# Attention of a hybrid transformer layer put in the program's own order, with steps and copies moved between places and engines

## Chip, cores and metric

The kernel runs on one core of a Trainium2 chip. The number that counts is the time of one execution on the device, in microseconds (us). Each kernel is also run once under the hardware profiler; the profile's times are from that one execution. The engines are PE (TensorE, matmuls and transposes), DVE (VectorE), ACT (ScalarE), POOL (GpSimd) and SP, which here only issues DMAs. Each engine takes its own instructions one after the other and waits for others by semaphores.

## The reference

One layer: a modulated RMSNorm, a projection to two groups of heads (attention, and a gated MLP over chunks), an output projection with a gated residual, then a mixture of 16 experts. All is fp32. The part that matters here is the attention over 1024 latent and 256 context tokens, 8 query heads in 2 groups of 4 that share a key and value head of 64 columns:

```python
def block(qb):
    s = jnp.einsum('bqkgd,bskd->bkgqs', qb, k).astype(jnp.float32) * scale
    p = jax.nn.softmax(s, axis=-1).astype(v.dtype)
    return jnp.einsum('bkgqs,bskd->bqkgd', p, v)
...
mix_l = jnp.concatenate([gqa_attend(ql, k_all, v_all),
                         spatial_gating(hl, w_gm, v_gain, w_s, b_s)], axis=-1)
xl_new = xl + gt1 * (mix_l @ w_out)
```

## The kernel before

Products are made from fp32 values split in two parts that PE multiplies apart: a high part (`whi`, `ph`: a rounded copy) and a low part (`wlo`, `pl`: the value less the high part). A split is a copy on ACT or DVE and a subtraction on DVE or POOL.

The queries of all heads are computed first. Then the attention runs over 16 **units** `u`: 8 blocks of 128 queries, 2 groups of 4 heads each. A unit has 10 **steps** `kt`, one for each 128 of the 1280 keys. Step `i = 10 u + kt` of the loop at L827 holds:

- `scores` (L740): two matmuls into the PSUM tile `st` (L745, L746), 128 keys by 512 columns (4 heads of 128 queries), the exponential on ACT into `pf` (L748, four buffers), and the two parts of the probabilities: `ph`, a copy on ACT (L751) or DVE (L753), and `pl`, a subtraction on POOL (L755).
- up to three pieces of `head(u + 1)` (L628), the preparation of the next unit. It is a generator, and each `yield` ends a piece. For the first group of a block it doubles the queries into the tile `qd` (L634; here called QD); four transposes turn them (L640, tile `tp`); ACT copies the result to `QA` (L643, one of the tiles named HL), DVE subtracts to `QB` (L644). Then the maximum of the scores of each query is found: 8 products of 512 keys (L652) and 4 half ones (L659) into the PSUM tile `ap`, which has two buffers, each followed by a maximum on DVE (L654, L662); L665 takes the maximum over all, four transposes (L669) turn it into a row, and ACT copies it (L671) where the second score matmul of the next unit (L746) reads it, so that the maximum is subtracted in the product.
- `values` (L758) of the step five earlier (`LAG`): six matmuls of 256 columns (L768) into the PSUM tile `po`, which also hold the sums of the probabilities. After a unit's last one it is divided: two copies on ACT (L773, L774), a reciprocal (L775) and two products (L777, L778) on DVE.
- `next(side)`: from unit 3 on and every sixth step, a piece of the work for the stages behind: `gates` (L726), and `w_out` (L782), which loads a quarter of the out-projection's weights into `raw`, multiplies 128 rows by the gate (L789 on DVE) and splits them (L147 on ACT, L148 on DVE). The last quarter is multiplied only.

The order of instructions is set in two ways. The stage before the attention and the stages after it stand in a `manual_schedule`: each engine gets its instructions in the order in which the program issues them. The attention doesn't: there a scheduler places the instructions of every engine before the run. The rotation of the last block of queries (L840) is tied behind the first reciprocals by `issue_after`.

Of the kernel before, what the change touches and what calls it, by code (L numbers as in the profile page):

```python
# [47 lines left out]
def layer(ctx: ExitStack, tc: tile.TileContext, a, out, dbg=None):  # L48
# [69 lines left out]
    QD = [kvp.tile([P, NQ, 2, HD], F32, name="qd")]  # L118
# [430 lines left out]
    def q_gain(t):  # L549
        if t < NT - 1:  # L550
            qn = pq_.tile([P, NQ, HD], F32, name="vv", bufs=2)
        else:

            qn = pb_.tile([P, 512], F32, name="pf", bufs=4).rearrange("p (h d) -> p h d", h=NQ)
            qst["tmp"] = None
        qst[t] = qn
        if 3 <= t < NT - 1:
            for h in range(NQ):
                nc.scalar.activation(qn[:, h], ps[2 * NT + t][:, h * HD:(h + 1) * HD], AF.Copy,
                                     scale=qst["ss", t][:, h:h + 1])  # L560
        else:
            nc.vector.tensor_tensor(qn, ps[2 * NT + t].rearrange("p (h d) -> p h d", h=NQ),
                                    qst["ss", t].unsqueeze(2).to_broadcast([P, NQ, HD]), op=OP.mult)

    def q_rotate(t):
        qn = qst[t]
# [5 lines left out]
        ts = qst["tmp"][:, 512:1024] if t < NT - 1 else pb_.tile([P, 512], F32, name="pf", bufs=4)  # L572
        tv = ts.rearrange("p (h s i) -> p h s i", h=NQ, s=2)
        nc.vector.tensor_tensor(dv, xv, cosG[:, t, None].to_broadcast([P, NQ, 2, 32]), op=OP.mult)
        for i in range(2):
            nc.vector.tensor_tensor(tv[:, :, i, :], xv[:, :, 1 - i, :],
                                    sinG[:, t, None, 1 - i].to_broadcast([P, NQ, 32]), op=OP.mult)
        nc.vector.tensor_sub(dv[:, :, 0, :], dv[:, :, 0, :], tv[:, :, 0, :])
        nc.vector.tensor_add(dv[:, :, 1, :], dv[:, :, 1, :], tv[:, :, 1, :])

    for t in range(NT):
        s = 2 * NT + t
        at(s + 1, 0, q_norm, t)
        if t < NT - 1:
            at(s + 1, 4, q_gain, t)
            at(*((s + 1, 7) if t == NT - 2 else (s + 2, 1)), q_rotate, t)
# [41 lines left out]
    def head(u, psum, tags):  # L628
# [3 lines left out]
        if g == 0:  # L632
            qd = QD[0]
            nc.vector.tensor_copy(qd, qall[t].rearrange("p (h d) -> p h d", h=NQ).unsqueeze(2).to_broadcast(  # L634
                [P, NQ, 2, HD]))
            yield
        qd = QD[0]
        pq = ptile(0)
        for s, h in enumerate(HORD):
            nc.tensor.transpose(pq[:, s * P:(s + 1) * P], qd[:, g * QPK + h].rearrange("p a d -> p (a d)"), ident)  # L640
# [74 lines left out]
    psB = pool("psB", 1, space=PSUM)  # L715
    gt1b = pb_.tile([P, D], F32, name="gt1b")
# [23 lines left out]
    def scores(u, kt):  # L740
# [8 lines left out]
        ph = pb_.tile([P, 512], F32R, name="ph", bufs=LAG + 1)  # L749
        if kt in PH_ACT or (u == 0 and kt == 0):  # L750
            nc.scalar.copy(ph, pf)  # L751
        else:
            nc.vector.tensor_copy(ph, pf)  # L753
        pl = pb_.tile([P, 512], F32R, name="pl", bufs=LAG + 1)
        (nc.vector if kt in PL_DVE else nc.gpsimd).tensor_tensor(pl, pf, ph.bitcast(F32), op=OP.subtract)  # L755
        return ph, pl

    def values(u, k, ph, pl):  # L758
# [11 lines left out]
        if k == NK - 1:  # L770
            del U["po", u], U[u]
            rec = pb_.tile([P, 256], F32, name="rec", bufs=1)
            nc.scalar.copy(rec[:HD], po[HD:, 0:256])  # L773
            nc.scalar.copy(rec[HD:], po[:HD, 256:512])  # L774
            U["rec"] = nc.vector.reciprocal(rec, rec)  # L775
            dst = qall[t][:, g * 256:(g + 1) * 256]
            nc.vector.tensor_mul(dst[:HD], po[:HD, 0:256], rec[:HD])  # L777
            nc.vector.tensor_mul(dst[HD:], po[HD:, 256:512], rec[HD:])  # L778
# [3 lines left out]
    def w_out(cb, jh, later=None):  # L782
# [18 lines left out]
    PL_DVE, PH_ACT = (), (0, 2, 4, 5, 6, 8)  # L801
# [24 lines left out]
    C_AT = 12  # L826
    for i in range(NU * NK + LAG):  # L827
        u, kt = divmod(i, NK)
        if i < NU * NK:
            if kt == 0:  # L830
                nxt = head(u + 1, psB, (("tp", 2), ("ap", 2))) if u + 1 < NU else iter(())
            parts[i] = scores(u, kt)
            for _ in range(3 if kt < NK - 1 else 99):
                if next(nxt, 0) == 0:
                    break
        if u >= 3 and i % 6 == 0:
            next(side, None)
        if i == LAG + NK:
            with tc.issue_after(U["rec"].ins):
                q_rotate(NT - 1)  # L840
        if i >= LAG:
            values(*divmod(i - LAG, NK), *parts.pop(i - LAG))
        if i >= NU * NK - C_AT and (i - NU * NK + C_AT) % 2 == 0 and i < NU * NK - C_AT + 8:
            c_load(0, 1 + (i - NU * NK + C_AT) // 2)
    for _ in side:
        pass
    for t in range(NT):
        dump(f"o{t}", qall[t])
    psB.release()
# [755 lines left out]
```

## Time and profile before

| | before |
|---|---|
| time, median of 3 runs | 1797.2 us (1794.7 to 1797.37) |
| the profiled execution | 1797.9 us |
| its span, first to last instruction | 1795.7 us |
| mean granted clock of TensorE | 0.986 |
| PE, DVE, ACT, POOL busy, share of the span | 96%, 89%, 69%, 28% |

A row of a timeline gives start and duration, engine, the line of the kernel, the operation, what it writes and reads, and in brackets the time that its engine stood idle before it and what ended that. "PEld" is the load of a matmul's weights, which runs beside the matmul before it. In groups the number behind the bar is busy time in us and the mean of one in ns, and then the idle time before. Matmuls overlap: the distance of their starts, not their duration, is what one costs PE.

### The profile page before, as it was taken

What the parts mean: (1) busy time and instruction counts of PE and PEld (TensorE: products, weight loads), DVE (VectorE), ACT (ScalarE), POOL (GpSimd) and SP (SyncE); (2) the same over time, 40 slices, a digit from 0 to 9 for tenths busy, and PEclk for the clock granted to TensorE, in tenths of its full rate; (3) what the DMA queues carried; (4) which work ended last, traced back from release to release, by engine and by line L of the source; (5) the groups of instructions that cost most, each with busy time, mean ns of one, the idle gap of its engine ahead of it and who ended that gap; (6) DMA issues with size and microseconds to landing.
All of it is one profiled execution on the core that took longest, in us unless ns stands there. A gap on an engine that the chain in (4) does not pass through costs nothing.

```text
span 1795.7 us, 24620 instructions
## 1 busy us (share of the span) xinstructions
PE 1721.7 (96%) x8636; PEld 1417.9 (79%) x8636; DVE 1591.4 (89%) x2390; ACT 1246.4 (69%) x1675; POOL 507.3 (28%) x349
## 2 busy tenths in 40 slices
PE   7999999889999969999999999999999999999997
PEld 4888878778888858777778888888888888888885
DVE  7778788997758999999999999999999999999987
ACT  6542367657753348777777888887887888878875
POOL 1433468778851112333330110110101101101002
PEclk9999999899999989999999999999999999999999
DMA  9347200100025678999999999999999999999982
GB/s 352 100 154 233 81 1 1 47 1 1 13 95 204 230 270 317 348 365 365 345 371 379 392 382 383 388 380 382 387 385 377 387 385 373 390 383 377 376 303 94
DMA packets 204684, 484.65 MB, mean 270 GB/s; under 512 B 10416, under 2 KB 12816, under 8 KB 204560
## 3 DMA queue, kind: packets, MB, share of 16 engines
q1 hardware_dynamic: 200096, 466.83, 70.2%
q0 software_dynamic: 4464, 16.25, 3.6%
q8 instruction: 67, 1.10, 0.2%
q14 instruction: 57, 0.47, 0.1%
HBM read 462.60 MB, written 20.45 MB: 269 GB/s over the span
## 4 chain that ended last, share of the span: by engine, by line
PE 81%; DVE 12%; issue 2%; ACT 1%; POOL 1%; DMA 1%; POOLq 0%; DVEq 0%; ACTq 0%
PE p L1480 24%; PE p L1483 12%; PE py L1470 6%; PE py L1469 6%; PE py L1471 6%; PE po L768 4%; DVE wlo L148 3%; PE pj L691 2%; PE pj L693 2%; PE pj L692 2%; PE tp L1316 2%; PE ap L652 2%; PE st L746 2%; PE st L745 1%; PE pj L956 1%
## 5 line engine op out<-in xcount | busy, mean ns | idle before, releaser
L148 DVE TENSOR_TENSOR wlo<-raw,whi 128x1024 fp32r<-128x1024 f32 (+1 forms) x561 | 663.2, 1224 | 46.1 <-ACT whi L147 41.9
L147 ACT CAST whi<-raw 128x1024 fp32r<-128x1024 f32 (+1 forms) x595 | 597.4, 1020 | 124.0 <-PE p L1483 67.8
L755 POOL TENSOR_TENSOR pl<-pf,ph 128x512 fp32r<-128x512 f32 x160 | 215.2, 1362 | 59.0 <-DVE ph L753 23.5
L1480 PE MATMUL p<-whi,xb 128*128 128x512 f32 x512 | 204.9, 400 | 0.0
L1480 PE MATMUL p<-whi,xa 128*128 128x512 f32 x512 | 204.7, 400 | 0.0
L1480 PE MATMUL p<-wlo,xa 128*128 128x512 f32 x512 | 199.9, 390 | 0.0
L1480 PE MATMUL p<-wlo,xb 128*128 128x512 f32 x512 | 199.8, 390 | 0.0
L1470 PE MATMUL py<-wlo,thl 128*128 128x512 f32 x504 | 198.3, 394 | 0.0
L1469 PE MATMUL py<-whi,thl 128*128 128x512 f32 x504 | 197.6, 392 | 0.0
L1471 PE MATMUL py<-whi,thl 128*128 128x512 f32 x504 | 196.3, 389 | 0.0
L1483 PE MATMUL p<-whi,xb 128*128 128x512 f32 x512 | 158.1, 390 | 0.4 <-DVE xb L1436 0.4
L1483 PE MATMUL p<-whi,xa 128*128 128x512 f32 x512 | 158.0, 390 | 0.0
L748 ACT ACTIVATE pf<-st 128x512 f32<-128x512 f32 x160 | 95.4, 598 | 73.3 <-PE st L746 58.7
L148 DVE TENSOR_TENSOR wlo<-H,whi 128x1024 fp32r<-128x1024 f32 x104 | 129.1, 1267 | 8.5 <-ACT whi L147 7.5
L148 DVE TENSOR_TENSOR wlo<-gm,whi 128x1024 fp32r<-128x1024 f32 x108 | 130.5, 1229 | 5.7 <-ACT whi L147 5.3
L147 ACT CAST whi<-H 128x1024 fp32r<-128x1024 f32 x108 | 113.8, 1055 | 24.4 <-PE p L1483 18.5
L147 ACT CAST whi<-gm 128x1024 fp32r<-128x1024 f32 x108 | 112.8, 1053 | 16.3 <-PE py L1471 8.4
L1334 POOL DMA_INDIRECT acc<-ye,idx x15 | 38.1, 2539 | 289.8 <-DVE ye L1331 289.8
L1483 PEld LDWEIGHTS p<-whi,xb 128*128 128x128 f32 x512 | 96.0, 188 | 21.6 <-DVE xb L1436 0.8
L1483 PEld LDWEIGHTS p<-whi,xa 128*128 128x128 f32 x512 | 96.1, 188 | 20.9
L1469 PEld LDWEIGHTS py<-whi,thl 128*128 128x128 f32 x504 | 94.6, 188 | 21.5
L1480 PEld LDWEIGHTS p<-wlo,xa 128*128 128x128 f32 x512 | 96.3, 188 | 18.9 <-DVE wlo L148 0.4
(410 smaller groups left out, 3716.0 us busy)
## 6 DMA issues: line engine op xcount, KB each, us to landing
raw<-in_w_dram SPq DMA_DIRECT2D x272, 1024.0 KB, 8.2
H<-in_w_dram SPq DMA_DIRECT2D x54, 1024.0 KB, 7.8
gm<-in_w_dram SPq DMA_DIRECT2D x54, 1024.0 KB, 8.7
raw<-in_w_mod_dram SPq DMA_DIRECT2D x64, 256.0 KB, 3.2
raw<-in_w_mod_dram SPq DMA_DIRECT2D x4, 1024.0 KB, 7.6
raw<-in_w_in_dram SPq DMA_DIRECT2D x16, 256.0 KB, 3.7
raw<-in_w_out_dram SPq DMA_DIRECT2D x4, 1024.0 KB, 5.0
xr<-in_x_dram SPq DMA_DIRECT2D x8, 512.0 KB, 6.0
```

The costliest lines, as they stand in the source:

```text
L147: nc.scalar.copy(hi, src)
L148: (eng or nc.vector).tensor_tensor(lo, src, hi.bitcast(F32), op=OP.subtract)
L652: nc.tensor.matmul(pa_, QA[:, h * P:(h + 1) * P], K1[:, g, pp * 512:(pp + 1) * 512], start=True, stop=True)
L748: nc.scalar.activation(pf, pst, AF.Exp, scale=HD ** -0.5)
L755: (nc.vector if kt in PL_DVE else nc.gpsimd).tensor_tensor(pl, pf, ph.bitcast(F32), op=OP.subtract)
L768: nc.tensor.matmul(po[:, sl], st[:, blk], mv[:, sl], start=(k == 0 and o == 0 and n == 0), stop=(k == NK - 1 and n == 2), skip_group_check ...
L1334: nc.gpsimd.indirect_dma_start(out=acc, out_offset=bass.IndirectOffsetOnAxis(ap=idx[:, e:e + 1], axis=0), in_=G["ye"], in_offset=None, com ...
L1469: nc.tensor.matmul(PY[e][cb], th, hi[:, sl], start=fst, stop=False)
L1470: nc.tensor.matmul(PY[e][cb], th, lo[:, sl], start=False, stop=False)
L1471: nc.tensor.matmul(PY[e][cb], tl, hi[:, sl], start=False, stop=lst)
L1480: nc.tensor.matmul(p, xh[:, j, :], w[:, jj, :], start=(j == 0 and w is pr[0]), stop=False)
L1483: nc.tensor.matmul(p, xl[:, j, :], pr[0][:, jj, :], start=False, stop=(j == DJ - 1))
```

## The change

- The attention gets a `manual_schedule` (mB): on every engine the order is now the program's.
- `halves` is cut off from `scores` and is called one step later. `ph` is copied on ACT in eight steps of ten where it was six, and `ph` and `pl` have five buffers each where they had six.
- `head` copies QD on ACT, and ends a piece behind the copy of QA.
- The division is a generator `divide`, in three pieces: ACT's copies, the reciprocal a step later behind the head's pieces, the two products another step later.
- `side` has the last rotation of queries in front (four pieces), is called every fourth step from unit 1 on, and `w_out` is cut in pieces of half the size (the product and ACT's copy; the subtraction).
- The last queries' tiles `qn` and `qt` have space of their own and no longer take turns with `pf`.

```diff
-            nc.vector.tensor_copy(qd, qall[t].rearrange("p (h d) -> p h d", h=NQ).unsqueeze(2).to_broadcast(
-                [P, NQ, 2, HD]))
+            nc.scalar.copy(QD, qall[t].rearrange("p (h d) -> p h d", h=NQ).unsqueeze(2).to_broadcast([P, NQ, 2, HD]))
             yield
...
         nc.scalar.copy(QA, pq)
+        yield
         nc.vector.tensor_sub(QB[:HD], pq[:HD], QA[:HD].bitcast(F32))
...
     psB = pool("psB", 1, space=PSUM)
+    mB = tc.manual_schedule()
+    mB.__enter__()
...
-        ph = pb_.tile([P, 512], F32R, name="ph", bufs=LAG + 1)
-        if kt in PH_ACT or (u == 0 and kt == 0):
+        return pf
+
+    def halves(u, kt, pf):
+        ph = pb_.tile([P, 512], F32R, name="ph", bufs=LAG)
+        if kt in PH_ACT:
             nc.scalar.copy(ph, pf)
         else:
             nc.vector.tensor_copy(ph, pf)
-        pl = pb_.tile([P, 512], F32R, name="pl", bufs=LAG + 1)
-        (nc.vector if kt in PL_DVE else nc.gpsimd).tensor_tensor(pl, pf, ph.bitcast(F32), op=OP.subtract)
+        pl = pb_.tile([P, 512], F32R, name="pl", bufs=LAG)
+        nc.gpsimd.tensor_tensor(pl, pf, ph.bitcast(F32), op=OP.subtract)
...
+    def divide(u):
+
+        t, g = divmod(u, NKV)
+        po = U.pop(("po", u))
+        del U[u]
+        rec = pb_.tile([P, 256], F32, name="rec", bufs=1)
+        nc.scalar.copy(rec[:HD], po[HD:, 0:256])
+        nc.scalar.copy(rec[HD:], po[:HD, 256:512])
+        yield
+        nc.vector.reciprocal(rec, rec)
+        yield
+        dst = qall[t][:, g * 256:(g + 1) * 256]
+        nc.vector.tensor_mul(dst[:HD], po[:HD, 0:256], rec[:HD])
+        nc.vector.tensor_mul(dst[HD:], po[HD:, 256:512], rec[HD:])
+        yield
...
             if later is None:
-                split_to(*w_part(pair, jj), raw[:, jj, :])
+                hi, lo = w_part(pair, jj)
+                nc.scalar.copy(hi, raw[:, jj, :])
+                yield
+                nc.vector.tensor_sub(lo, raw[:, jj, :], hi.bitcast(F32))
             yield
...
-    PL_DVE, PH_ACT = (), (0, 2, 4, 5, 6, 8)
+    PH_ACT = (0, 1, 2, 4, 5, 6, 8, 9)
...
+    fresh, fin = None, iter(())
+    side = chain(q_rotate(NT - 1), side)
     for i in range(NU * NK + LAG):
         u, kt = divmod(i, NK)
+        pf = None
         if i < NU * NK:
             if kt == 0:
                 nxt = head(u + 1, psB, (("tp", 2), ("ap", 2))) if u + 1 < NU else iter(())
-            parts[i] = scores(u, kt)
-            for _ in range(3 if kt < NK - 1 else 99):
-                if next(nxt, 0) == 0:
-                    break
-        if u >= 3 and i % 6 == 0:
+            pf = scores(u, kt)
+
+        if fresh:
+            parts[i - 1] = halves(*divmod(i - 1, NK), fresh)
+        fresh = pf
+        for _ in range(3 if kt < NK - 1 else 99):
+            if next(nxt, 0) == 0:
+                break
+        next(fin, None)
+        if i >= NK and i % 4 == 2:
             next(side, None)
-        if i == LAG + NK:
-            with tc.issue_after(U["rec"].ins):
-                q_rotate(NT - 1)
         if i >= LAG:
-            values(*divmod(i - LAG, NK), *parts.pop(i - LAG))
+            u, k = divmod(i - LAG, NK)
+            values(u, k, *parts.pop(i - LAG))
+            if k == NK - 1:
+                fin = divide(u)
+                next(fin)
```

How the instructions stand now is shown at three places, with the row's number on its engine and the line of the kernel that it belongs to (the changed kernel's lines are one to thirteen higher there).

First, PE in the unit that prepares unit 11, around the transposes of the maxima (L669, in the changed kernel L670). Before:

```order
1940 L745 MATMUL st<-HL_110,K_102 128x512
1941 L669 MATMUL tp<-ident,m_4433 128x128 x4
1942 L746 MATMUL st<-HL_110 128x512
1943 L768 MATMUL po<-ph,HL_382 128x256
1944 L768 MATMUL po<-ph,HH_383 128x256
1945 L768 MATMUL po<-pl,HL_382 128x256
1946 L768 MATMUL po<-ph,HL_382 128x256
1947 L768 MATMUL po<-ph,HH_383 128x256
1948 L768 MATMUL po<-pl,HL_382 128x256
1949 L745 MATMUL st<-HL_110,K_102 128x512
1950 L746 MATMUL st<-HL_382,HL_110 128x512
```

After:

```order
1897 L748 MATMUL st<-HL_110,K_102 128x512
1898 L749 MATMUL st<-HL_110 128x512
1899 L670 MATMUL tp<-ident,m_4441 128x128 x2
1900 L774 MATMUL po<-ph,HL_382 128x256
1901 L774 MATMUL po<-ph,HH_383 128x256
1902 L774 MATMUL po<-pl,HL_382 128x256
1903 L774 MATMUL po<-ph,HL_382 128x256
1904 L774 MATMUL po<-ph,HH_383 128x256
1905 L774 MATMUL po<-pl,HL_382 128x256
1906 L748 MATMUL st<-HL_110,K_102 128x512
1907 L749 MATMUL st<-HL_110 128x512
1908 L670 MATMUL tp<-ident,m_4441 128x128 x2
```

Before, the four transposes stand in the unit's last step; the next unit's first scores (the second one reads `HL_382`) follow at rows 1949 and 1950, with one step's values between. After, the transposes come two by two at rows 1899 and 1908, in the unit's steps 6 and 7, and two whole steps more of scores and values (not shown) follow before the next unit's.

Second, DVE for the same unit, from the subtraction L644 (L645) to the maximum over all, L665 (L666). Before:

```order
406 L644 TENSOR_TENSOR HL_382<-tp,HL_110 64x512
407 L654 TENSOR_REDUCE mx<-ap 128x1 x4
408 L753 CAST ph<-pf 128x512
409 L662 TENSOR_REDUCE mx<-ap 128x2
410 L654 TENSOR_REDUCE mx<-ap 128x1 x4
411 L775 RECIPROCAL rec<-rec 128x256
412 L662 TENSOR_REDUCE mx<-ap 128x2
413 L777 TENSOR_TENSOR H_2084<-po,rec 64x256
414 L778 TENSOR_TENSOR H_2084<-po,rec 64x256
415 L665 TENSOR_REDUCE m_4433<-mx 128x4
```

After:

```order
382 L645 TENSOR_TENSOR HL_382<-tp,HL_110 64x512
383 L655 TENSOR_REDUCE mx<-ap 128x1 x3
384 L802 TENSOR_TENSOR raw<-raw,gt1b 128x512
385 L655 TENSOR_REDUCE mx<-ap 128x1
386 L759 CAST ph<-pf 128x512
387 L663 TENSOR_REDUCE mx<-ap 128x2
388 L655 TENSOR_REDUCE mx<-ap 128x1 x4
389 L786 RECIPROCAL rec<-rec 128x256
390 L663 TENSOR_REDUCE mx<-ap 128x2
391 L666 TENSOR_REDUCE m_4441<-mx 128x4
392 L789 TENSOR_TENSOR H_2081<-po,rec 64x256
393 L790 TENSOR_TENSOR H_2081<-po,rec 64x256
```

The reciprocal stands ahead of the last half maximum in both. After, a product of the out-projection's weights (L802) stands among the maxima, and the division's two products have gone behind the maximum over all.

Third, the copy QD for unit 12: before on DVE, after on ACT. Before, DVE:

```order
402 L665 TENSOR_REDUCE m_4232<-mx 128x4
403 L753 CAST ph<-pf 128x512
404 L634 COPY qd<-H_2084 128x1024
405 L753 CAST ph<-pf 128x512
406 L644 TENSOR_TENSOR HL_382<-tp,HL_110 64x512
407 L654 TENSOR_REDUCE mx<-ap 128x1 x4
```

After, ACT:

```order
373 L751 ACTIVATE pf<-st 128x512 x2
374 L757 CAST ph<-pf 128x512
375 L751 ACTIVATE pf<-st 128x512
376 L757 CAST ph<-pf 128x512
377 L636 COPY qd<-H_2081 128x1024
378 L805 CAST whi<-raw 128x512
379 L751 ACTIVATE pf<-st 128x512
380 L757 CAST ph<-pf 128x512
381 L643 CAST HL_110<-tp 128x512
```

Before, the copy stands ahead of the maxima for unit 11. After, it is issued in the first step of unit 11, behind an exponential (L751) and a copy of `ph` (L757), and a copy of out-projection weights (L805) follows it; the transposes of QD follow it on PE.

## Rows read from the trace of the kernel before

**Rows 1.** The page: busy time of PE, share, instructions
```profile
PE 1721.7 (96%) x8636; PEld 1417.9 (79%) x8636; DVE 1591.4 (89%) x2390; ACT 1246.4 (69%) x1675; POOL 507.3 (28%) x349
```

**Rows 2.** Windows: two stretches of the attention, busy time of each engine
```profile
core 0: us, PE busy (x) PEld busy (x) DVE busy (x) ACT busy (x) POOL busy (x), PEclk, DMA share, GB/s
283.50:403.50 120.00, 103.66 (x626) 90.42 (x625) 107.34 (x147) 75.25 (x135) 86.98 (x62) 0.93 0.06 18
403.50:498.50 95.00, 93.60 (x601) 81.54 (x601) 72.64 (x116) 68.38 (x120) 77.68 (x61) 1.00 0.02 7
```

**Rows 3.** Timeline: L671, once a unit; start us, us, engine, line, names
```profile
234.59 0.58 ACT L671 CAST HL<-tp 64x512 fp32r<-64x512 f32 x1 [0.25 <-PE tp L669]
283.49 0.58 ACT L671 CAST HL<-tp 64x512 fp32r<-64x512 f32 x1
403.53 0.58 ACT L671 CAST HL<-tp 64x512 fp32r<-64x512 f32 x1
498.55 0.58 ACT L671 CAST HL<-tp 64x512 fp32r<-64x512 f32 x1
```

**Rows 4.** Timeline: PE and one exponential in the quiet stretch
```profile
432.40 0.39 PE L746 MATMUL st<-HL 128*128 128x512 f32 x1
432.63 0.28 PE L768 MATMUL po<-ph,HL 128*128 128x256 f32 x1
432.75 0.28 PE L768 MATMUL po<-ph,HH 128*128 128x256 f32 x1
432.89 0.60 ACT L748 ACTIVATE pf<-st 128x512 f32<-128x512 f32 x1
434.77 0.60 PE L669 MATMUL tp<-ident,m 128*128 128x128 f32 x4
435.13 0.48 PE L746 MATMUL st<-HL 128*128 128x512 f32 x1
```

**Rows 5.** Groups, 400 to 480 us, DVE; busy us, mean ns
```profile
L654 DVE TENSOR_REDUCE mx<-ap 128x1 f32<-128x512 f32 x40 | 26.1, 678 | 0.8
L753 DVE CAST ph<-pf 128x512 fp32r<-128x512 f32 x20 | 11.0, 552 | 12.1 <-ACT pf L748 12.0
L775 DVE RECIPROCAL rec<-rec 128x256 f32<-128x256 f32 x6 | 10.5, 1742 | 0.0
```

**Rows 6.** Groups, ACT, 400 to 480 us; last row 1000 to 1400
```profile
L748 ACT ACTIVATE pf<-st 128x512 f32<-128x512 f32 x51 | 30.5, 598 | 21.0 <-PE st L746 20.4
L751 ACT CAST ph<-pf 128x512 fp32r<-128x512 f32 x31 | 19.3, 621 | 1.0
L643 ACT CAST HL<-tp 128x512 fp32r<-128x512 f32 x5 | 2.9, 581 | 0.0
L147 ACT CAST whi<-raw 128x1024 fp32r<-128x1024 f32 x202 | 210.2, 1054 | 39.5 <-PE p L1483 25.0 <-PE py L1471 14.4
```

**Rows 7.** Timeline: waits of PE, the copy QD, DVE's chain
```profile
251.33 0.41 PEld L669 LDWEIGHTS tp<-ident,m 128*128 128x128 f32 x4 [0.99 <-DVE m L665]
422.18 1.84 DVE L634 COPY qd<-H 128x1024 f32<-128x1024 f32 x1 [2.35 <-PE tp L640]
424.28 0.67 DVE L644 TENSOR_TENSOR HL<-tp,HL 64x512 fp32r<-64x512 f32 x1
425.60 0.50 PE L652 MATMUL ap<-K,HL 128*128 128x512 f32 x1 [0.67 <-DVE mx L654]
434.19 0.17 DVE L665 TENSOR_REDUCE m<-mx 128x4 f32<-128x12 f32 x1
```

**Rows 8.** Groups, 300 to 400 us, DVE; and line L789, min/median/max ns
```profile
L789 DVE TENSOR_TENSOR raw<-raw,gt1b 128x512 f32<-128x512 f32 x16 | 20.9, 1344 | 0.2 <-ACT gt1b L724 0.2
L148 DVE TENSOR_TENSOR wlo<-raw,whi 128x512 fp32r<-128x512 f32 x12 | 12.3, 1046 | 0.0
L789 DVE TENSOR_TENSOR raw<-raw,gt1b x16: 676/1750/1783, 301.6 to 386.4; 128x512 f32<-128x512 f32 x16
```

**Rows 9.** Waits, 300 to 400 us; us in all, times, longest
```profile
PEld ap L652 <- DVE mx L654: 12.6, 5, 3.8
```

More of the change, by code (lines that the diff above doesn't have):

```diff
@@ L117, in layer @@
     cosG, sinG = (kvp.tile([P, NT, 2, 32], F32, name=n) for n in ("cosG", "sinG"))
-    QD = [kvp.tile([P, NQ, 2, HD], F32, name="qd")]
+    QD = kvp.tile([P, NQ, 2, HD], F32, name="qd")
     pa = pool("pa", 1)
@@ L552, in q_gain @@
         else:
-            qn = pb_.tile([P, 512], F32, name="pf", bufs=4).rearrange("p (h d) -> p h d", h=NQ)
+            qn = pb_.tile([P, 512], F32, name="qn").rearrange("p (h d) -> p h d", h=NQ)
             qst["tmp"] = None
@@ L571, in q_rotate @@
         dv = qall[t].rearrange("p (h s i) -> p h s i", h=NQ, s=2)
-        ts = qst["tmp"][:, 512:1024] if t < NT - 1 else pb_.tile([P, 512], F32, name="pf", bufs=4)
+        ts = qst["tmp"][:, 512:1024] if t < NT - 1 else pb_.tile([P, 512], F32, name="qt")
         tv = ts.rearrange("p (h s i) -> p h s i", h=NQ, s=2)
         nc.vector.tensor_tensor(dv, xv, cosG[:, t, None].to_broadcast([P, NQ, 2, 32]), op=OP.mult)
+        yield
         for i in range(2):
@@ L585, in layer @@
             at(s + 1, 4, q_gain, t)
[L586 removed]
+            at(*((s + 1, 7) if t == NT - 2 else (s + 2, 1)), lambda t: list(q_rotate(t)), t)
     def small_loads():
@@ L632, in head @@
         if g == 0:
-            qd = QD[0]
-            nc.vector.tensor_copy(qd, qall[t].rearrange("p (h d) -> p h d", h=NQ).unsqueeze(2).to_broadcast(
-                [P, NQ, 2, HD]))
+            nc.scalar.copy(QD, qall[t].rearrange("p (h d) -> p h d", h=NQ).unsqueeze(2).to_broadcast([P, NQ, 2, HD]))
             yield
-        qd = QD[0]
         pq = ptile(0)
         for s, h in enumerate(HORD):
-            nc.tensor.transpose(pq[:, s * P:(s + 1) * P], qd[:, g * QPK + h].rearrange("p a d -> p (a d)"), ident)
+            nc.tensor.transpose(pq[:, s * P:(s + 1) * P], QD[:, g * QPK + h].rearrange("p a d -> p (a d)"), ident)
             yield
@@ L769, in values @@
                                  stop=(k == NK - 1 and n == 2), skip_group_check=True)
[L770 to L778, printed above, removed]
+    def divide(u):
[7 more added lines that the diff above has]
+        nc.vector.reciprocal(rec, rec)
+        yield
+        dst = qall[t][:, g * 256:(g + 1) * 256]
+        nc.vector.tensor_mul(dst[:HD], po[:HD, 0:256], rec[:HD])
+        nc.vector.tensor_mul(dst[HD:], po[HD:, 256:512], rec[HD:])
+        yield
     wob = [[None, None], [None, None]]
@@ L831, in layer @@
                 nxt = head(u + 1, psB, (("tp", 2), ("ap", 2))) if u + 1 < NU else iter(())
-            parts[i] = scores(u, kt)
-            for _ in range(3 if kt < NK - 1 else 99):
-                if next(nxt, 0) == 0:
-                    break
-        if u >= 3 and i % 6 == 0:
+            pf = scores(u, kt)
[7 more added lines that the diff above has]
+        if i >= NK and i % 4 == 2:
             next(side, None)
-        if i == LAG + NK:
-            with tc.issue_after(U["rec"].ins):
-                q_rotate(NT - 1)
         if i >= LAG:
-            values(*divmod(i - LAG, NK), *parts.pop(i - LAG))
+            u, k = divmod(i - LAG, NK)
[3 more added lines that the diff above has]
+                next(fin)
         if i >= NU * NK - C_AT and (i - NU * NK + C_AT) % 2 == 0 and i < NU * NK - C_AT + 8:
             c_load(0, 1 + (i - NU * NK + C_AT) // 2)
+    for _ in fin:
+        pass
     for _ in side:
@@ L848, in layer @@
         dump(f"o{t}", qall[t])
+    mB.__exit__(None, None, None)
     psB.release()
```

1 line of the change is left out of this document (added).

## The prediction

> **What bounds the kernel now.** I read the page first: TensorE (PE) is busy 96% of the span [rows 1], so the question in any stage is what holds PE up there. The change lies in the attention, whose units begin at about 235 us [rows 3]. The stage table splits it [rows 2]: in 283.5 to 403.5 us DVE is busy 107 of 120 us, PE 104, at a granted clock of 0.93; in 403.5 to 498.5 us DVE has slack (73 of 95 us), PE is busy 94 of 95 us, at 1.00. The ends of the units are marked by the copy L671, once a unit [rows 3]. Six units take 403.53 - 283.49 = 120.0 us in the first stretch (20.0 each) and 498.55 - 403.53 = 95.0 us in the second (15.8 each); fifteen take 498.55 - 234.59 = 264.0 us. The first stretch is the one with the 16 products L789 and 12 subtractions L148 on DVE [rows 8], and its first wait is PE for a maximum on DVE [rows 9].
>
> What PE could do at best I take from its starts [rows 4]. Two score matmuls follow each other at 0.23 us, value matmuls (256 columns) at 0.12, and the four transposes of the maxima push the next start back by 0.36, 0.09 each. A step (2 scores, 6 values) is 1.18 us. A unit is 10 steps (11.8), 8 wide maximum products (1.85), 4 half ones (0.47) and 8 transposes (0.72): 14.85 us. The quiet units at 15.8 hold one microsecond of waiting each; more than that a better order can't give them.
>
> **The change part by part.** The edit that carries the forecast is none of the three in its name. It is that the attention now stands in the program's order on every engine, so that PE, which takes its instructions in order, meets each wait where the code puts it. Where PE's next instruction waits, the ready ones behind it wait too: at 251.33 the transposes of the maxima held PE 0.99 us for L665, and at 425.60 a product held it 0.67 us for a maximum [rows 7].
>
> *Transposes of the maxima.* Before, they stood in the unit's last step, one step ahead of the next unit's scores; now in steps 6 and 7, with the values of step 6 and three whole steps behind them (first two pieces of order). What they wait for is a chain on DVE that starts when the unit's Q is copied (L643): a subtraction (0.67) and at the end L665 (0.17) [rows 7], between them 8 maxima and 2 of the same length for the half products, a reciprocal (1.74) and a probability copy (0.55) [rows 5]. The maxima have a mean of 0.68 but overlap a little, so I take 0.65: 0.67 + 8 x 0.65 + 2 x 0.68 + 0.55 + 1.74 + 0.17 = 9.7 us. The trace agrees: from L644 at 424.28 to L665 at 434.19 are 9.9 us [rows 7], with 0.8 us of the division's products in between, which now come after. The reciprocal stands ahead of the last half maximum before and after (third and fourth piece), so it stays in the chain. PE has, from the first product to these transposes, the values of steps 2 to 5 (4 x 0.72), the scores of steps 3 to 6 (4 x 0.46), 8 x 0.23 and 4 x 0.12: 7.1 us. In the old order the rest of DVE's chain was covered by the next steps' scores and values; that cover now stands behind the wait. PE therefore waits at least 9.7 - 7.1 = 2.6 us a unit. The products come three in a row with two buffers, and when PE is held at the third, DVE in turn runs dry a little later; following one unit of each kind product by product, I get 0.9 to 1.2 us of such gaps, so 10.7 us in all and a wait of 3.6 us a unit, in two parts: some 1.5 to 2 us before products and about 2 us before the transposes.
>
> *Q's copy.* In step 1 ACT has the exponential (0.60) and a probability copy (0.62) ahead of L643 (0.58) [rows 6]. From the end of that step's scores that is 0.25 until ACT sees the result (432.40 to 432.89 less one start of 0.23 [rows 4]), then 1.80, and 0.1 of hand-over: 2.15 us. PE has a transpose or two, the values and the next scores, 1.3 us. Wait: 0.85 us a unit.
>
> *QD on ACT.* Before, DVE made it most of a unit ahead (fifth piece; at 422.18 it took 1.84 us, and DVE waited 2.35 us before it [rows 7]). Now ACT makes it in step 0 of every second unit, behind that step's exponential and a probability copy (sixth piece), and PE's transposes behind the scores wait for it. No row shows it on ACT; the nearest are 128x512 at 0.62 and 128x1024 at 1.05 [rows 6], and I take the latter, having its size. 0.25 + 0.60 + 0.62 + 1.05 + 0.1 = 2.6 us, seven times in fifteen units: 18 us. The bounds are 2.2 us with the smaller row and nothing if ACT came to it early, which it can't while the exponential ahead waits for scores.
>
> *Out-projection weights.* Their work stays the same (16 products, 12 subtractions on DVE, 12 copies on ACT); every 4th step now issues one half of what every 6th did, from unit 3 to 14. About one step a unit, eleven in all, falls between L643 and L665, in DVE's chain; the others fall where DVE has five microseconds to spare and cost nothing under that cover. A step is 1.34 or 1.05 us [rows 8]; up to 0.4 fills the gaps counted above. 11 x 0.8 = 9 us, with bounds of 0 (all in gaps) and 11 x 1.75 = 19 (the median of L789).
>
> On those two durations the Trainium skill, "SBUF — State Buffer", section "Who interferes with whom", has a rule: GpSimd and a DVE operation with two SBUF inputs exclude each other for a whole instruction. The trace agrees in that L789 averages 1.34 us where a maximum of as many elements from PSUM takes 0.68. By that rule every step that meets a subtraction of L755 takes the longer time, and the term would be its upper bound, 19, not 9.
>
> *Probability parts one step late, two more copies on ACT, divide in three pieces.* Copying in ACT adds 2 x 0.62 us a unit; ACT was busy 75 of 120 us, 12.5 a unit [rows 2], and comes to some 14 of 20 with QD's half; that is hidden behind PE's waits, and where it isn't it is the 0.85 above. The low parts come a step later, with four steps left before their values, and the four pf buffers lose a step of slack; POOL was busy 87 of 120 us at a like pace [rows 2], so I cost this at nothing, and at 1 us a unit if POOL falls behind. The rotation of the last Q is spread over four steps: under 1 us. The last unit, without products, is as before. SP's queue keeps its order.
>
> **The sum.** 15 x (14.85 + 3.6 + 0.85) = 289.5, plus 18, plus 9: 316.5 us against 264.0, so 52.5 us more. The profiled execution took 1797.9 us (span 1795.7 and 2.2 around it); that gives 1850.4. The median of the runs is 0.7 lower, within their spread: I say 1850. The attention ends with a dependent stage, so nothing takes this back later.
>
> **The rivals.**
> *The weights' relief decides (faster).* If PE met its waits in the new order no later than in the quiet stretch, the six units at 20.0 would fall to 15.8 and nothing would be lost: 25 us, 1773. For it: [rows 2] blame exactly the weights' stretch, and DVE gets lighter by QD and two copies. It decides from the point where DVE's chain is shorter than PE's 7.1 us; the chain is 9.7, and that speaks against it. 9%.
> *The waits share one cover.* While PE waits for the maxima, ACT catches up, and the waits for Q and QD shrink to nothing. Then 15 x 18.45 + 9 = 285.8: 1820. Against it: both hang on scores issued after the wait, not on ACT's backlog. 9%.
> *The clock falls too.* At 0.93 [rows 2] PE's work in a unit is 16.0 instead of 14.85, 15 x 1.1 = 17 us more: 1867, and with POOL late at 1 us a unit 1882. For it: PE would work three quarters of the time, as in the first stretch. Against it: there PE waited up to 3.8 us at a time [rows 9], here 2.6 at most. 12%.
> *No net change.* Waits of 2.7 us a unit instead of one, and the weights' excess gone, would come out even. Nothing in the rows gives that number. 3%.
>
> **How the numbers follow.** The forecast has 67%, with a range of its own of 1828 to 1872 (gaps of 0 to 2 us a unit are 15 us either way, the weights' step 9 to 10). The range is 1814 to 1884: it takes in the shared cover and the clock, and leaves out the faster case. About 0.2% is what a measurement of this kernel can tell from no change; faster has 9%, the same 2%, slower 89%.
>
> **What would show it.** L671 would come every 19 to 21.5 us from unit 1 to 14, the same where weights are worked on as where not. PE would wait at the transposes of the maxima for L665, about 2 us fifteen times; at the first transpose of every second unit for the copy QD, about 2.6 us; at products for maxima, 1.5 to 2 us a unit; at the first product for Q's copy, just under 1. DVE would be busy about two thirds. The forecast is wrong if L671 comes every 16 us, or if PE's longest waits are for POOL or for exponentials.

## The result, and the profile after

The changed kernel takes 1856.7 us (median of 4 runs, 1853.86 to 1857.54) where the kernel before, beside it, took 1797.1 us: ratio 1.033, 95% interval 1.0313 to 1.0346. The forecast was 1850, in a range of 1814 to 1884. Lines of the changed kernel are one to thirteen higher than those of before (L671 is L672, L652 is L653, L659 is L660, L665 is L666, L669 is L670).

The page of the changed kernel, busy time by engine; it answers to [rows 1]:

```profile
span 1853.8 us, 24717 instructions
PE 1735.7 (94%) x8636; PEld 1415.6 (76%) x8636; DVE 1556.5 (84%) x2350; ACT 1261.8 (68%) x1715; POOL 498.5 (27%) x349
```

PE and ACT are busy 14 and 15 us longer than before, DVE and POOL 35 and 9 us less, and the span is 58.1 us longer: most of the time went into waiting. The same two windows as in [rows 2]:

```profile
283.50:403.50 120.00, 94.67 (x564) 77.04 (x562) 69.49 (x109) 69.15 (x128) 69.38 (x54) 0.97 0.03 9
403.50:498.50 95.00, 75.12 (x457) 61.61 (x457) 55.76 (x86) 58.80 (x110) 59.28 (x46) 0.98 0.04 12
```

In the first, DVE fell from 107 to 69 us. Part of that is the relief one could have hoped for, part only the slower pace (109 instructions where there were 147); PE fell from 104 to 95. In the second PE fell from 93.60 to 75.12 of 95 us. No engine is near full in either, which points to the order; the experiments test it. The marks of the units, as in [rows 3], six of the sixteen:

```profile
238.60 0.58 ACT L672 CAST HL<-tp 64x512 fp32r<-64x512 f32 x1
252.72 0.58 ACT L672 CAST HL<-tp 64x512 fp32r<-64x512 f32 x1
...
470.13 0.58 ACT L672 CAST HL<-tp 64x512 fp32r<-64x512 f32 x1
493.12 0.58 ACT L672 CAST HL<-tp 64x512 fp32r<-64x512 f32 x1
512.42 0.58 ACT L672 CAST HL<-tp 64x512 fp32r<-64x512 f32 x1
...
554.76 0.58 ACT L672 CAST HL<-tp 64x512 fp32r<-64x512 f32 x1
```

Fifteen units take 316.2 us, where they took 264.0 and where the forecast said 316.5. The rest of the 58.1 lies outside them: the first mark comes 4.0 us later, and from the last mark to the end are 1299.0 us in place of 1297.15. Nothing is given back later.

What PE waits for shows at its weight loads (PEld), which stop before the matmuls do. Their waits between 235 and 560 us (us in all, times, longest us):

```profile
PEld tp L670 <- DVE m L666: 27.5, 15, 2.2
PEld tp L640 <- ACT qd L636: 18.5, 7, 2.6
PEld ap L660 <- DVE mx L655: 13.9, 16, 1.0
PEld ap L653 <- DVE mx L655: 12.2, 23, 1.0
PEld ap L653 <- ACT HL L643: 11.9, 12, 1.5
PEld ap L653 <- DVE mx L663: 7.4, 8, 1.0
PEld ap L653 <- PE ap L653: 6.4, 7, 1.0
```

Together 97.8 us; the units' 316.2 less fifteen times 14.85 us, the forecast's figure for PE's work, leave 93.5. Before, the same floor left 41.2 of 264.0, so 52.2 of the 93.5 are new. By PE's own rows, which begin later, the same places make 64.6 us; the rows of PEld are thus a measure of where PE is held, and not of what each place costs to the microsecond. Each names its place: the transposes of the maxima for L666, the transposes of QD for ACT, the products for maxima, the first product for Q's copy. In the timeline of PE one of each of the first two kinds looks like this, with the idle time and its releaser in brackets, and the copy QD on ACT beside it:

```profile
467.29 0.43 PE L670 MATMUL tp<-ident,m 128*128 128x128 f32 x2 [1.77 <-DVE m L666]
473.77 1.05 ACT L636 COPY qd<-H 128x1024 f32<-128x1024 f32 x1
474.87 0.44 PE L640 MATMUL tp<-ident,qd 128*128 128x128 f32 x2 [2.20 <-ACT qd L636]
```

And DVE's chain that ends at L666, from the subtraction to the division's reciprocal and the last half maximum:

```profile
456.17 0.68 DVE L645 TENSOR_TENSOR HL<-tp,HL 64x512 fp32r<-64x512 f32 x1 [3.92 <-ACT HL L643]
...
464.74 1.74 DVE L786 RECIPROCAL rec<-rec 128x256 f32<-128x256 f32 x1
466.40 0.63 DVE L663 TENSOR_REDUCE mx<-ap 128x2 f32<-128x512 f32 x1
467.06 0.17 DVE L666 TENSOR_REDUCE m<-mx 128x4 f32<-128x12 f32 x1
```

From 456.17 to 467.06, start to start, are 10.9 us, PE's next transposes start at 467.29, and DVE stood idle for 3.92 us before the chain began. DVE isn't short of time; its work comes too late in the unit.

### The profile page after: what moved, and what is told of

The parts are those of the page before. It is cut to its first block, busy times and chain, and to the rows that moved or that the text cites. A ratio compares the mean times of both kernels' runs of the same rounds, so it can differ in the third digit from the quotient of the medians.

```text
span 1853.8 us, 24717 instructions
## 1 busy us (share of the span) xinstructions
PE 1735.7 (94%) x8636; PEld 1415.6 (76%) x8636; DVE 1556.5 (84%) x2350; ACT 1261.8 (68%) x1715; POOL 498.5 (27%) x349
## 4 chain that ended last, share of the span: by engine, by line
PE 78%; DVE 13%; ACT 3%; issue 3%; DMA 1%; POOL 0%; DVEq 0%; POOLq 0%; SPq 0%; ACTq 0%
PE p L1508 24%; PE p L1511 12%; PE py L1498 6%; PE py L1497 6%; PE py L1499 6%; PE po L774 4%; DVE wlo L148 2%; PE pj L692 2%; PE pj L694 2%; PE pj L693 2%; PE tp L1344 2%; DVE mx L655 2%; DVE rec L786 1%; PE st L749 1%; PE st L748 1%
## 5 line engine op out<-in xcount | busy, mean ns | idle before, releaser
L148 DVE TENSOR_TENSOR wlo<-raw,whi 128x1024 fp32r<-128x1024 f32 (+1 forms) x549 | 652.4, 1231 | 45.9 <-ACT whi L147 41.8
L147 ACT CAST whi<-raw 128x1024 fp32r<-128x1024 f32 (+1 forms) x583 | 589.6, 1028 | 116.3 <-PE p L1511 68.6
L761 POOL TENSOR_TENSOR pl<-pf,ph 128x512 fp32r<-128x512 f32 x160 | 208.7, 1321 | 123.9 <-ACT ph L757 108.6
L751 ACT ACTIVATE pf<-st 128x512 f32<-128x512 f32 x160 | 95.9, 599 | 93.2 <-PE st L749 78.2
L147 ACT CAST whi<-H 128x1024 fp32r<-128x1024 f32 x108 | 113.8, 1055 | 24.4 <-PE p L1511 18.5
L1511 PEld LDWEIGHTS p<-whi,xb 128*128 128x128 f32 x512 | 96.1, 188 | 21.5 <-DVE xb L1464 0.8
L1511 PEld LDWEIGHTS p<-whi,xa 128*128 128x128 f32 x512 | 96.1, 188 | 20.9
L1497 PEld LDWEIGHTS py<-whi,thl 128*128 128x128 f32 x504 | 94.6, 188 | 21.5
```

Source lines behind the costliest of these rows:

```text
L147: nc.scalar.copy(hi, src)
L148: (eng or nc.vector).tensor_tensor(lo, src, hi.bitcast(F32), op=OP.subtract)
L751: nc.scalar.activation(pf, pst, AF.Exp, scale=HD ** -0.5)
L761: nc.gpsimd.tensor_tensor(pl, pf, ph.bitcast(F32), op=OP.subtract)
L1497: nc.tensor.matmul(PY[e][cb], th, hi[:, sl], start=fst, stop=False)
L1511: nc.tensor.matmul(p, xl[:, j, :], pr[0][:, jj, :], start=False, stop=(j == DJ - 1))
```

## The experiments

Theory: PE meets four dependences where the program puts them, each with its own price, and they add. Rivals: the waits cover one another; or the loss comes from the work that was moved to ACT, and the order has little to do with it. Every kernel was timed beside the kernel before (1796.4 to 1797.3 us, medians). Unless said otherwise, an edit is made in the changed kernel.

**1. All edits, but the scheduler's order.**

```diff
-    mB = tc.manual_schedule()
-    mB.__enter__()
...
-    mB.__exit__(None, None, None)
```

> The changed kernel with the attention left to the scheduler again, every other edit kept (late halves, eight copies on ACT, QD on ACT, divide in pieces, weights spread). Theory (the program's order alone costs the time): PE's waits at the transposes of the maxima and of QD go, the time falls by 50 us or more, to between 1775 and 1805 us, and if the spread of the weights' steps is worth anything it ends under the kernel before. Rival (the copies moved to ACT and the late halves cost it): ACT is as loaded as now, the time stays above 1835.

1797.4 us, ratio 1.0005 (0.9995 to 1.0014). With the scheduler the other edits together are worth nothing, and without the program's order the whole loss is gone. The `manual_schedule` orders all engines at once; no run takes it from PE alone. The weights' steps stay drawn together, and the window of [rows 2] reads nearly as before, with DVE at 100 us:

```profile
283.50:403.50 120.00, 102.41 (x639) 90.25 (x638) 100.26 (x133) 84.68 (x154) 86.74 (x62) 0.94 0.06 19
```

**2. The order alone.** In the kernel before:

```diff
+    mB = tc.manual_schedule()
+    mB.__enter__()
...
-            with tc.issue_after(U["rec"].ins):
-                q_rotate(NT - 1)
+            q_rotate(NT - 1)
...
+    mB.__exit__(None, None, None)
```

> The kernel before with one edit of the change: the attention in the program's order (the last rotation of queries issued where the program has it). Theory: the maxima's transposes again stand in steps 6 to 8, behind a chain on DVE that here also holds the division's two products, 0.8 us more a unit, and the weights' pieces with their wait for ACT's copy, while QD on DVE has no queue ahead of it; about 45 us more than before, 1835 to 1860. Rival (the other edits cost the time): within 10 us of the kernel before, 1790 to 1807.

1893.0 us, ratio 1.0531 (1.0513 to 1.0548), above every number expected. The waits of PEld, 235 to 560 us:

```profile
PEld tp L669 <- DVE m L665: 45.6, 12, 5.9
PEld ap L652 <- DVE mx L654: 31.3, 45, 2.9
PEld tp L640 <- DVE qd L634: 13.4, 7, 2.5
```

and of DVE in the same stretch, of which the expectation had counted only the second, the weights':

```profile
DVE ph L755 <- ACT pf L750: 98.9, 46, 3.8
DVE wlo L148 <- ACT whi L147: 11.8, 12, 2.5
DVE rec L777 <- ACT rec L776: 7.2, 9, 0.8
```

Here DVE itself is held up in order: a probability copy stands behind its own exponential, a weights' subtraction behind its copy, the reciprocal behind ACT's, with the maxima queued behind. The wait at the transposes grows to 5.9 us. So the order costs 96 us by itself, and in this order the change's other edits give 36 of these back.

The granted clock has a part in that. From the first mark to the last (the copy of the maxima, once a unit), in the changed kernel, here, and in experiment 5, with the clock as the third number from the end:

```profile
238.60:554.80 316.20, 250.25 (x1480) 202.93 (x1481) 188.66 (x290) 187.17 (x346) 192.38 (x147) 0.97 0.03 9
234.90:592.30 357.40, 271.46 (x1479) 216.72 (x1478) 217.81 (x333) 177.36 (x312) 196.06 (x149) 0.92 0.03 8
236.20:504.10 267.90, 240.94 (x1483) 197.95 (x1484) 190.83 (x289) 186.16 (x347) 195.76 (x148) 1.00 0.03 11
```

PE was granted 0.92 on average here (1 is its upper level, 2.4 GHz, and 0.5 the lower, 1.2 GHz) and 0.97 in the changed kernel, and was busy 271.46 and 250.25 us with as many matmuls. So of the 41.2 us by which the units are longer here, some 21 go with slower matmuls and some 20 with waits. What lowers the clock was not tested, and no run holds it fixed.

**3. The transposes of the maxima two steps later, four together.**

```diff
+        for _ in range(4 + g if u else 0):
+            yield
         pmx = ptile(0)
         for h in range(QPK):
...
-            yield
+            if u == 0 or h == QPK - 1:
+                yield
```

> The changed kernel with the four transposes of the maxima issued together in step 8, with two steps of scores and values in front of them that now stand behind. Theory: PE's wait for L666, 22 to 27 us in fifteen units, is covered by those steps; 1830 to 1837. Rival (PE's wait only shows that DVE or ACT bounds the unit): the wait comes back at the products or at Q's copy, and the time stays within 5 us of 1857.

1836.0 us (1830.36 to 1841.28), 20.7 less. The four runs lie 11 us apart, and their clocks with them (0.982 in the slowest, 0.992 in the fastest), so the 20.7 is good to some 5 us. The row for L666 is gone, and the others stay:

```profile
PEld tp L640 <- ACT qd L636: 19.2, 7, 2.9
PEld ap L660 <- DVE mx L655: 13.6, 16, 1.0
```

A wait of 27.5 us at the weight loads (21.9 by PE's own rows) was worth 20.7.

**4. QD a unit earlier on ACT.** The copy is taken out of the head of even units and issued at the end of the head before (double(t) is the copy L636):

```diff
-            nc.scalar.copy(QD, qall[t].rearrange("p (h d) -> p h d", h=NQ).unsqueeze(2).to_broadcast([P, NQ, 2, HD]))
...
         U[u] = (QA, QB)
+        if g and t + 1 < NT:
+            yield
+            double(t + 1)
```

> The changed kernel with QD copied on ACT in step 7 or 8 of the unit before, behind the copy of the maxima, instead of in the first step of the unit. Theory: PE's wait for QD, 15 to 18 us in seven units, goes whole, since the copy then ends more than a step ahead of its transposes; 1838 to 1842. Rival (ACT is full, and the copy delays the exponentials as much): within 4 us of 1857.

1835.8 us (1834.3 to 1837.42), 20.9 less than the changed kernel, for a row of 18.5 (15.4 by PE's own rows). ACT still makes the copy, so it was its place that cost.

**5. Both moves, and the copies to `ph` behind the head's pieces of their step.** The edits of 3 and 4, and:

```diff
-        if fresh:
-            parts[i - 1] = halves(*divmod(i - 1, NK), fresh)
-        fresh = pf
         for _ in range(3 if kt < NK - 1 else 99):
             if next(nxt, 0) == 0:
                 break
+        if fresh:
+            parts[i - 1] = halves(*divmod(i - 1, NK), fresh)
+        fresh = pf
```

> The changed kernel with three moves in the order and nothing else: the four transposes of the maxima together in step 8, Q's double written on ACT one unit earlier, and the copies to ph and pl issued behind the head's pieces of the step, so that Q's copy stands ahead of a copy to ph on ACT. Theory (each stall is a dependence of its own, met by TensorE in its order, and they add): 1856.7 - 20.7 (late transposes) - 20.9 (early QD) - 6 to 9 for Q's copy = 1806 to 1810; no row for L640 or L666 above 0.5 us mean among TensorE's waits, and the row for Q's copy below 6 us. Rival (the stalls cover one another, so that taking both away gains little over one): 1826 to 1836, with the row for the products of the maxima behind DVE grown to 30 us or more.

1806.5 us (1804.55 to 1806.97): 50.2 less, where the sum of the two moves alone is 41.6, so the third is worth about 9. The stalls add, within the spread of these runs. Two signs were missed: the row for Q's copy fell at PE itself (6.7 to 2.7 us) more than at the weight loads (11.9 to 9.1, where below 6 was expected), and at the transposes of QD three waits with a mean of 0.9 us are left, where 0.5 at most was expected. The three rows for maxima grew a little, from 33.5 to 37.9 us. And of the 48.3 us by which the units got shorter, some 9 go with the clock, which was 1.00 here (rows in 2), and some 39 with the waits.

**6. The best order.** The moves of 5 and more: one piece of the head at a time, with half a step's values between two of them; the reciprocal and the quotient's products behind the maxima; the weights in pieces of one instruction; no new piece in unit 0's head.

```diff
+        next(nxt, None)
...
+        if i >= NK and i % 3 == 1:
             next(side, None)
...
+            values(u, k, *parts.pop(i - LAG), lambda: next(nxt, None))
+            if kt in (6, 7):
+                next(fin, None)
```

> Program order still, with the moves of the run with three moves, and further: the pieces of the head spread over the steps with a step's matmuls of the values between the two, the reciprocal and the products of the quotient behind the maxima of the head, the weights of the out-projection in pieces of one instruction (product, copy on ACT, subtraction) so that no engine's queue holds a piece that waits for another engine's piece of the same step, and no further piece in the head of unit 0. Theory: all waits of TensorE for the head go but some 0.3 us a unit: fifteen units at 15.5 us or so are 233 to 245 us beside 264.0 of before, and the time 1775 to 1792. Rival (the scheduled order is already as good as any order by hand, since DVE's and POOL's work for the weights still stands somewhere): 1797 or above, with a unit at 17.5 us or more.

1773.7 us, ratio 0.9875 (0.9858 to 0.9891): faster than both kernels. Its marks, and the first of the two windows:

```profile
232.82 0.58 ACT L689 CAST HL<-tp 64x512 fp32r<-64x512 f32 x1 [0.25 <-PE tp L684]
471.26 0.58 ACT L689 CAST HL<-tp 64x512 fp32r<-64x512 f32 x1
```

```profile
283.50:403.50 120.00, 117.11 (x770) 105.12 (x769) 96.33 (x147) 97.03 (x182) 104.00 (x78) 1.00 0.06 19
```

Fifteen units in 238.4 us, 15.9 each, with the weights' products spread from 285.0 to 472.3 us. PE's longest group of waits up to 500 us is:

```profile
PE ap L661 <- DVE mx L663: 4.7, 6, 2.8
```

**7. The probability parts in their own step.** The values go four steps behind, so that they have as many buffers and as much room behind the parts as before the edit.

```diff
-    LAG = 5
+    LAG = 4
...
-            pf = scores(u, kt)
-
-        if fresh:
-            parts[i - 1] = halves(*divmod(i - 1, NK), fresh)
-        fresh = pf
+            parts[i] = halves(u, kt, scores(u, kt))
```

> The changed kernel with the probability parts made in their own step again and the values four steps behind in place of five, so that the parts still lie four steps ahead of the matmuls that read them (the buffers are as many). Theory: a copy to ph on ACT now stands directly behind its exponential, and on DVE and POOL waits for it, with the head's pieces queued behind: 1860 to 1885, TensorE's row for Q's copy (ACT) and the rows for the maxima grown. Rival (the step of delay is worth nothing, as the forecast had it): 1852 to 1860.

1883.9 us (1881.62 to 1888.05), 27 more: the rival, which is the forecast's own view, falls. DVE's waits for exponentials, in the changed kernel and then here:

```profile
DVE ph L759 <- ACT pf L751: 4.6, 5, 1.5
```

```profile
DVE ph L759 <- ACT pf L751: 38.5, 27, 3.4
```

A copy that stands directly behind its exponential holds DVE, and the maxima behind it. PE's row for the half products grew with it, from 13.9 to:

```profile
PEld ap L660 <- DVE mx L655: 25.3, 14, 2.4
```

The values' lag moved along with it, so the 27 us are those of both. The clock is in them too: over the units it was 0.92, and PE was busy 266.93 us for the 250.25 of the changed kernel, some 17 of the 33 us by which the units got longer in the profiled executions.

**8. Six copies on ACT.**

```diff
-    PH_ACT = (0, 1, 2, 4, 5, 6, 8, 9)
+    PH_ACT = (0, 2, 4, 5, 6, 8)
```

> The changed kernel with the copies to ph divided as before (six of ten on ACT in place of eight). Theory: neither ACT nor DVE is the bound, the stalls are in the order, so that 0.69 us twice a unit back on DVE is felt only where a maximum stands behind it: 1853 to 1866. Rival (ACT's load of copies holds up Q's copy and QD): 1835 to 1850.

1852.7 us (1850.33 to 1855.03), against 1853.86 to 1857.54 of the changed kernel. The two ranges overlap and the number falls just below the theory's range and short of the rival's gain; the two more copies on ACT cost between nothing and some 4 us. The rows of PEld show both sides of it: with six copies the wait for QD is 14.8 us in place of 18.5, and that of the products (L653) for L655 is 17.0 in place of 12.2.

**9. The best order, placed by the scheduler** (the edit of 1, in the kernel of 6).

> The kernel with the best order so far (1773.7 us) without the attention's manual_schedule, so that the scheduler places its instructions. Theory: the gain lies in the order of the instructions alone, and the scheduler makes its own of them: 1790 to 1800, with the weights' steps drawn together again and PE waiting up to 4 us at products for maxima there. Rival (the gain lies in the cut of the work, half-size pieces and the spread, that any order can use): 1770 to 1780.

1790.2 us, ratio 0.9964 (0.995 to 0.9978), 16.5 more than by hand. The scheduler draws the weights together again, so that DVE and PE share the first window as in [rows 2], with one wait on top between 235 and 560 us:

```profile
283.50:403.50 120.00, 104.27 (x657) 93.68 (x656) 101.79 (x138) 88.34 (x162) 91.95 (x66) 0.94 0.06 18
```

```profile
PEld ap L661 <- DVE mx L663: 22.1, 10, 5.3
```

About 7 us of the gain do survive under the scheduler.

**10. The weights in a bunch** (in the kernel of 6).

```diff
-        if i >= NK and i % 3 == 1:
+        if u >= 3 or (u == 1 and i % 2 == 0):
```

> The kernel with the best order so far, with one edit: the pieces of the out-projection's weights are issued at every step from unit 3 on, where they were issued at every third from unit 1 on, so that they stand in some four units, about as closely as the scheduler puts them in the kernel before. Theory (the spread pays once nothing else holds the order up): DVE has about 11 us of other work in a unit and gets 7 to 9 us of weights on top in these four units, 18 to 20 us against 15.9; 3 us each, so 1781 to 1790. Rival (DVE's slack and the buffers even it out): 1772 to 1777.

1781.3 us (1780.98 to 1784.28), 7.6 more. PE's weight loads wait 13.5 us for maxima at L661 where they waited 6.5. In this order the spread of the weights is worth that much; what it is worth in the changed kernel, among the other stalls, no run tested.

**11. The division ahead of the values again** (in the kernel of 6).

```diff
-            if kt in (6, 7):
-                next(fin, None)
...
+        next(fin, None)
+        if i >= NK and i % 3 == 1:
```

> The kernel with the best order so far, with one edit: the reciprocal and the two products of the quotient are issued in steps 5 and 6 ahead of the values, as in the changed kernel, in place of behind the maxima in steps 6 and 7. Theory (the reciprocal's 1.74 us stands in DVE's chain, and the chain is what the products and the transposes wait for): 0.5 to 1.5 us a unit, 1781 to 1796. Rival (with the head's pieces one by one and the transposes late, the chain has the room): 1772 to 1777.

1784.1 us (1783.4 to 1785.35), 10.4 more, and the wait at the transposes is back, although they come late:

```profile
PEld tp L684 <- DVE m L675: 20.9, 14, 2.0
```

The reciprocal stands in the chain, as the forecast had counted it; the quotient's two products moved with it, and the runs don't part the two.

**12. Unit 0's head without the new piece.**

```diff
         nc.scalar.copy(QA, pq)
-        yield
+        if u:
+            yield
```

> The changed kernel with one edit: the new end of a piece behind Q's copy holds from unit 1 on only, so that in the stage ahead of the attention the pieces of unit 0's head fall on the places that were set for them, and the copy of its maxima no longer stands behind the split of V on ACT. Theory (the head of unit 0 slid by a piece, and TensorE's wait of 2.3 us for that copy, with the 0.7 us for its maxima, is lost time): 1853 to 1855, the wait for L672 gone, and the copy beside the last projection matmul as before. Rival (this wait covers for ACT's and DVE's backlog at the start of unit 0, which is met a little later all the same): 1856 to 1858.

1853.6 us (1852.19 to 1855.16). In the changed kernel this copy stood behind the split of V on ACT, and PE waited for it:

```profile
237.33 1.25 ACT L147 CAST HL<-V 128x1280 fp32r<-128x1280 f32 x1
238.60 0.58 ACT L672 CAST HL<-tp 64x512 fp32r<-64x512 f32 x1
239.32 0.48 PE L749 MATMUL st<-HL 128*128 128x512 f32 x1 [2.30 <-ACT HL L672]
```

Here it comes earlier, and of the wait 0.9 us, for another step, is left:

```profile
235.70 0.58 ACT L673 CAST HL<-tp 64x512 fp32r<-64x512 f32 x1 [0.25 <-PE tp L671]
```

The place of the 2.3 us is shown. What taking it away is worth is not: the median fell by 3.1 us as expected, but the runs of the two kernels overlap, and in the profiled executions the first mark comes 2.9 us earlier and the last only 0.9 (553.83 against 554.76). PE's wait at the products (L653) for the maxima of L655 was 4.6 us with 0.6 at most in the changed kernel; here, with the lines one higher, it is:

```profile
PE ap L654 <- DVE mx L656: 6.1, 8, 2.0
```

So the rival, a backlog that is met a little later, holds at least in part.

## Why the prediction was right, and where it was off

*The edit that carries it.* Right: without the program's order the time is that of before (experiment 1), with nothing but that order it is 96 us above (2).

*Transposes of the maxima.* Forecast about 2 us fifteen times; measured 27.5 us in 15 (21.9 in 14 by PE's own rows), and taking them away gave 20.7. The chain was 10.9 us at 456.17 where 9.7, or 10.7 with gaps, was worked out.

*QD on ACT.* 1.05 us for the copy, from a row of another operation of that size, was what it took, and 18 us for the seven waits stand against 18.5. The 0.1 us of hand-over in that sum came from no row; here it is 0.05, from the copy's end at 474.82 to the transposes at 474.87.

*Q's copy.* 0.85 us a unit is 12.75; the row says 11.9, and the third move of experiment 5 was worth about 9.

*Products for maxima.* 1.5 to 2 us a unit are 22 to 30; the three rows that name DVE say 33.5 at the weight loads and 20.6 at PE itself. So the term was a little too small by one measure and about right by the other.

*Weights.* Priced at 1.34 and 1.05 us a step, eleven of them in DVE's chain, 9 us in all. Eleven did fall between L645 and L666, but each took 0.68 us, and they seem to have stood in gaps: the chain of the one unit with no such step and no rotation in it (from 308.76) takes 11.4 us, those of the five later units of its kind, with a step, 11.0 to 11.8. That puts the term near its lower bound of nothing, though one unit is a thin comparison. All steps on DVE, in the chain and out of it, 235 to 560 us (busy us, mean ns):

```profile
L802 DVE TENSOR_TENSOR raw<-raw,gt1b 128x512 f32<-128x512 f32 x16 | 15.4, 964 | 0.1
L807 DVE TENSOR_TENSOR wlo<-raw,whi 128x512 fp32r<-128x512 f32 x12 | 11.6, 963 | 0.0
```

A product took 0.68 us at 458.65, when POOL had just ended two subtractions (begun at 455.86, 2.70 us), and 1.80 where a subtraction on POOL ran all the while:

```profile
323.24 2.99 POOL L761 TENSOR_TENSOR pl<-pf,ph 128x512 fp32r<-128x512 f32 x2 [1.67 <-ACT ph L757]
323.28 1.80 DVE L802 TENSOR_TENSOR raw<-raw,gt1b 128x512 f32<-128x512 f32 x1
```

The mutual exclusion that the Trainium skill ("SBUF — State Buffer", "Who interferes with whom") describes fits this pair. In the slower order POOL stands idle more (busy 69 us of the first window, 87 before), and the median of L802 fell from 1.75 to 0.69 us, so the upper bound of 19 us, at 1.75 a step, was not met.

*Hits that rest on a balance.* That 316.5 meets 316.2 so closely is luck. The first unit took 14.1 us where a mean of 19.3 was assumed, since it has no values in its first five steps; from 324 us on they alternate, 23.0 with QD in them and 19.3 without (470.13, 493.12, 512.42), where 19 to 21.5 was said. DVE was busy 58 to 59% of the two windows, not two thirds.

*The step that was off* is "probability parts one step late, two more copies on ACT, divide in three pieces", costed at nothing. As a cost that nearly held: no row of PE's waits names these steps, and only the two copies show, in the wait for QD (8). But as changes they are not neutral. Taken back, the delay costs 27 us together with the lag of five steps and the lower clock (7), and without all edits beside the order the time is 36 us higher (2), where the expectation, about 45 us for the order alone, had counted on less than half of the 96. The forecast met the total since it followed the changed order as it stood and didn't build it up from the order alone. It also left out a wait: in the changed kernel ACT's copy of the weights waits for DVE's product, with exponentials queued behind it on ACT. What that costs is not shown:

```profile
ACT whi L805 <- DVE raw L802: 16.0, 10, 2.2
```

*Outside the units.* The forecast had nothing here; measured are 4.0 us ahead, 2.3 of them at the wait of experiment 12, and 1.9 behind, whose cause was not looked for. Together they are 5.9 of the 6.7 us between 1850 and 1856.7.

*The rivals.* Waits sharing a cover: no, they added (3, 4, 5). The clock: over the units it was 0.97 before and after, so it adds nothing to the change; with the order alone it fell, to 0.92 (2). The weights' relief: it didn't decide; 7.6 us of it show in the order of experiment 6 (10), where little else waits.

## What to carry to other kernels

When a loop is taken from a scheduler into the program's order, list for each engine what waits and what is queued behind it, and place a consumer at least as many steps behind its producer as the producer's whole chain takes; here the moves were then worth about what the waits said, and they added up. A yield, a delay or an earlier copy costs nothing to write and here moved almost the same work from 1893 to 1774 us. Look at the granted clock before the whole of a difference is put down to waits: in two of the orders here the matmuls were slower too. And read the gain of a spread in an order in which little else waits; it was measured here only in such a one.

## What the runs showed of the hardware

The copy that doubles QD takes 1.05 us on ACT in all eight units of the changed kernel (1047 to 1048 ns). On DVE it took 1.84 us at one place of the kernel before [rows 7], and between 0.68 and 1.85 over its eight; in the order-only kernel it was on DVE as steady as on ACT, and shorter (least, median, longest ns):

```profile
L634 DVE COPY qd<-H x8: 678/679/682, 202.8 to 552.0; 128x1024 f32<-128x1024 f32 x8
```

So the move to ACT costs 0.4 us against DVE's best and saves 0.8 against its worst. Which of these DVE shows depends on the order around the copy; what lengthens it was not tested.

The granted clock differed with the order: with the same matmuls it was 0.92, 0.97 and 1.00 over the units of the order-only kernel, the changed kernel and that of experiment 5, and TensorE's busy time was 271, 250 and 241 us. The kernel before had 0.97 too, with fewer waits, so the waits alone don't set it.
